# Neighbourhood attention by head pairs on two row halves, another split of the accumulator banks, and two more gate chunks ahead of attention, in a two-layer transformer trunk on one core

## The chip, the cores and the metric

The kernel runs on one core of a Trainium2 chip. The metric is the device time of one execution in microseconds (us). Before the change the median of three runs is 1344.7 us (1344.02 to 1344.84).

A core has five engines that run beside each other, each through its own instructions in order: TensorE (PE, with its weight loads listed as PEld), VectorE (DVE), ScalarE (ACT), GpSimd (POOL) and SyncE (SP), which here issues most of the loads. They wait for each other through semaphores. TensorE writes to PSUM, which has 8 banks of 128 × 512 f32 values.

## The reference

A trunk of two layers over 256 context tokens and 256 latent tokens, width 1024. Each layer has a mixer with two attentions in parallel and a feed-forward part. Cut to what matters:

```python
def mixer_proj(h, w_in, ...):
    p = h @ w_in                      # gates | c_q | c_kv | k_r | na q,k,v
    mq = rms_norm(c_q, g_qa) @ w_uq   # 8 heads of 96 (64 + 32 rotary)
    kv = rms_norm(c_kv, g_kva) @ w_ukv
    nq, nk, nv = ...                  # 8 heads of 64
    return gate_logits, mq, mk, mv, nq, nk, nv

# latent attention (MLA): latent queries see context + latent keys
y_mla = softmax(mq mk^T / sqrt(96)) mv
# neighbourhood attention (NA): a 4 x 16 window of the 4 x 64 grid, with a
# learned bias per head, and all context keys, in one softmax
s_win = nq k_win^T / 8 + bias;  s_ctx = nq k_ctx^T / 8
y_na  = softmax([s_win, s_ctx]) [v_win, v_ctx]
g = sigmoid(gate_logits)
y = (g[:1024] * (y_mla @ w_mla_o) + g[1024:] * (y_na @ w_na_o)) @ w_out
x = x + gate * y
x = x + gate2 * (relu(h2 @ w_ff1)**2 @ w_ff2)
```

In layer one the context tokens go through the same steps, seeing context alone. Layer two is the last, so only the latent tokens have queries, gates and a feed-forward part there.

## The kernel before

All inputs are f32. A weight tile is loaded by SP (`raw`), rounded by ScalarE to a high part (`whi`, L127), and VectorE makes the rest (`wlo`, L128). A product is three matmuls, high × high, low × high and high × low (`mm3`, L101 to L103), in a reduced f32 format that the trace calls fp32r. The four groups of 128 tokens are two of context (0, 1) and two of latent (2, 3); layer two takes queries from groups 2 and 3 only, so its gate matmuls have 256 columns where layer one's have 512.

The PSUM banks are shared by tag: A has three, B two, C two, D one (`BANKS`, L55). A tile waits until an earlier tile of its tag has been read.

Each layer runs through these stages: projections of `w_in` (c_kv, c_q, then keys, values and queries of MLA); the gate chunks that come ahead, `NG0 = 6` of 16 (a chunk is 128 of the gates' 2048 columns, 24 matmuls, drawn in the trace as `psB<-h,whi` ahead of attention and as `psA<-h,whi` later); MLA; the remaining `chunk_na` projections of NA; NA; the remaining gates; `w_mla_o`, `w_na_o`, `w_out`; the feed-forward part. The code is written for a scheduler that orders each engine's instructions by priority and by what is ready in its own plan. It draws projections in between MLA's steps and gate chunks in between NA's.

Attention before goes by head. `attend` (L816) takes the heads two at a time; for each, `prep` brings the transposed and split queries and keys (once per pair in NA), and in NA the head's bias: four loads on SP (L766), then an addition of the window mask on GpSimd (L767), into one of two `bias` buffers. `soft` (L784) goes over the tokens: three score matmuls into a bank of tag B, for latent tokens the bias added by VectorE (L778), the maximum (L787), the exponential on ScalarE (L796), reciprocal and scaling on VectorE (L798, L799), then transpositions of P on TensorE (L806) and the copies of the result (`PT`, L810 on ScalarE, L812 on VectorE). The value matmuls (L833) follow, head 1 and head 0 on the two column halves of the array. Head 1 of a pair starts after head 0. A head has 64 dimensions, so a score matmul of NA fills 64 of the array's 128 rows: head 0 of a pair lies on partitions 0 to 63 and head 1 on 64 to 127.

The context queries of layer one have 256 keys per token, the latent ones 512.

Of the kernel before, what the change touches and what calls it, by code (L numbers as in the profile page):

```python
# [37 lines left out]
NG0 = 6  # L38
# [7 lines left out]
def trunk(ctx: ExitStack, tc, t):  # L46
# [8 lines left out]
    BANKS = {"A": 3, "B": 2, "C": 2, "D": 1}  # L55
# [6 lines left out]
    def psx():  # L62
        cyc[0] += 1
        return ps("ABACBAC"[cyc[0] % 7])
# [316 lines left out]
    def load_xT(k):  # L381
        o = ps("AAABBABA"[k])
# [70 lines left out]
    for l in range(DEPTH):  # L453
# [16 lines left out]
        cqp = [ps("A"), ps("A"), ps("A"), ps("B"), ps("B"), ps("C") if l else ps("C")]  # L470
# [52 lines left out]
        def proj_b(load, nk, act_h, act_l, toks, N, evac, banks=("AA", "AA")):  # L523
# [3 lines left out]
            for p0 in range(0, len(toks), 2):  # L527
                pair = toks[p0:p0 + 2]
                outs = [ps(b)[:, :N] for b in banks[p0 // 2]]
                n = 0  # L530
                for wh, wl, ks in tiles:
                    for j, k in enumerate(ks):
                        for o, tk in zip(outs, pair):
                            cs = slice(tk * 128, (tk + 1) * 128)
                            mm3(o, act_h(k)[:, cs], act_l(k)[:, cs], wh[:, j], wl[:, j], n == 0, n == total - 1)
                        n += 1
                for o, tk in zip(outs, pair):
                    evac(tk, o)
# [31 lines left out]
        def rope(z, tab, lt, n):  # L570
# [7 lines left out]
            for half in range(2):  # L578
                zz = z[:, :, half * 16:(half + 1) * 16]
                aa = a[:, :, half * 16:(half + 1) * 16]  # L580
                bb = b[:, :, half * 16:(half + 1) * 16]
                nc.gpsimd.tensor_tensor(out=zz[:, :, 0:8], in0=aa[:, :, 0:8], in1=bb[:, :, 8:16], op=ALU.add)
                nc.gpsimd.tensor_tensor(out=zz[:, :, 8:16], in0=aa[:, :, 8:16], in1=bb[:, :, 0:8], op=ALU.add)
# [37 lines left out]
        proj_b(ckv_load, 3, H, Lo, [0, 1, 2, 3], KVL + RD, ckv_evac, ("CD", "AA"))  # L621
# [89 lines left out]

        gates(NG0, "B")

# [31 lines left out]
        na_pair = {}  # L745

        def prep_na(h):
            if h % 2 == 0:
                cs = slice(h * HD, (h + 2) * HD)
                o = ps("C")  # L750
                for tk in range(q0, 4):
                    nc.tensor.transpose(o[:, tk * 128:(tk + 1) * 128], nqk[:, tk, cs], rev if tk >= 2 else ident)
                qh, ql = qk_tile(), qk_tile()
                split_ps(qh[:, c_q], ql[:, c_q], o[:, c_q], gcn[:, l:l + 1])
                o = ps("C")
                for tk in range(4):
                    nc.tensor.transpose(o[:, tk * 128:(tk + 1) * 128], nqk[:, 4 + tk, cs], ident)
                kh, kl = qk_tile(), qk_tile()
                split_ps(kh, kl, o)
                na_pair[0] = (qh, ql, kh, kl)  # L760
            bias = ap.tile([128, 2, ROWS, GW], F32, tag="bias", name="bias", bufs=2)
            for row in range(ROWS):
                src = bass.AP(tensor=t["rpb"].tensor, offset=(l * NH + h) * RPB + (7 - row) * RW + 15 - (GW - 1),
                              ap=[[1, GW], [RW, ROWS], [1, GW]])
                pr = (row % 2) * 64
                nc.sync.dma_start(out=bias[pr:pr + 64, row // 2], in_=src)  # L766
            nc.gpsimd.tensor_tensor(out=bias.rearrange("p a i j -> p (a i) j"), in0=bias.rearrange("p a i j -> p (a i) j"),  # L767
# [48 lines left out]
        def attend(prep, score, vsel, ev, perm):  # L816
            groups = ([] if last else [([0, 1], LC, 0)]) + [([2, 3], TT, 1)]
            nxt = prep(0)
            for hp in range(NH // 2):
# [3 lines left out]
                for gi, (toks, K, st) in enumerate(groups):  # L823
# [6 lines left out]
                    for kt in range(nkt):  # L830
# [7 lines left out]
                        with tc.issue_after(first.ins):  # L838
                            av(0, ta)
# [260 lines left out]
```

## Time and profile before

| | us |
|---|---|
| median of 3 runs | 1344.7 |
| lowest, highest | 1344.02, 1344.84 |
| the profiled execution | 1344.34 |
| its span in the trace | 1342.6 |

The granted clock of TensorE averages 0.992 in it. The stages in that execution, by where the named instructions stand in the trace:

| us from the start | stage |
|---|---|
| 0 to 158 | layer one: modulation, norm, projections |
| 158 to 266 | MLA, with NA's projections in between |
| 280 to 369 | NA, with gate chunks in between |
| 369 to 486 | rest of the gates, `w_mla_o`, `w_na_o`, `w_out`, norm |
| to 843 | feed-forward |
| 843 to 926 | layer two: projections, six gate chunks |
| 926 to 989 | MLA |
| 989 to 1024 | rest of NA's projections |
| 1024 to 1090 | NA, with gate chunks in between |
| 1090 to 1145 | rest of the mixer |
| to the end | feed-forward |

In a row of the trace stands the start, the length, the engine, the line, the operation, the tiles (out<-in, buffer numbers left out) with rows and columns, and in brackets how long the engine stood idle before and what released it. TensorE works on several matmuls at once, so the length of one is more than what it adds; what it adds is read from one start to the next.

### The profile page before, as it was taken

The page shows a single profiled execution, that of the slowest core. Times are in us where ns is not written, and L with a number is a line of the kernel's source. Part 1 is how long each engine was busy: PE and PEld are TensorE (multiplying, and loading weights), DVE is VectorE, ACT ScalarE, POOL GpSimd, SP SyncE. Part 2 cuts the span into 40 slices and gives each one's busy share as a digit, 9 for nine tenths or more (in the row PEclk, how much of TensorE's full clock was granted, in tenths as well). Part 3 has the DMA queues.
Part 4 walks back from the last instruction along what each step waited for, and adds up shares of the span by engine and source line. Part 5 has one row for each costly group of instructions (what it writes and reads, how often), then busy time and mean ns, then how long its engine had stood idle before and what let it go on. Part 6 is the DMA issues. An engine that isn't in the chain of part 4 may idle for free.

```text
span 1342.6 us, 20389 instructions
## 1 busy us (share of the span) xinstructions
PE 1306.7 (97%) x7825; PEld 1098.5 (82%) x7825; DVE 863.4 (64%) x1462; ACT 586.5 (44%) x1061; POOL 275.8 (21%) x296
## 2 busy tenths in 40 slices
PE   6999999999999989999999999998999999999997
PEld 4698888976687868888888888898889789899896
DVE  4589377867885588887574334765854766755453
ACT  3455366445423344331423313564654544554442
POOL 3035403401005003210201100056040121221111
PEclk8999999999999999999999999999999999999999
DMA  9865411544477645465473344575134769656652
GB/s 277 285 151 165 151 32 32 157 113 85 93 261 235 202 144 165 150 187 173 133 212 96 101 125 150 167 191 150 32 87 97 121 216 273 170 163 189 189 187 94
DMA packets 245985, 208.01 MB, mean 155 GB/s; under 512 B 24496, under 2 KB 226992, under 8 KB 245504
## 3 DMA queue, kind: packets, MB, share of 16 engines
q1 hardware_dynamic: 235856, 190.16, 49.9%
q10 hardware_dynamic: 9520, 16.29, 3.4%
q8 instruction: 61, 1.00, 0.3%
q0 software_dynamic: 512, 0.27, 0.2%
q14 instruction: 36, 0.29, 0.1%
HBM read 195.15 MB, written 11.53 MB: 154 GB/s over the span
## 4 chain that ended last, share of the span: by engine, by line
PE 57%; issue 5%; DMA 2%; DVE 1%; POOL 1%; ACT 1%; SPq 0%; POOLq 0%; ACTq 0%; DVEq 0%
PE psA L103 8%; PE psA L102 8%; PE psA L101 8%; PE psB L101 5%; PE psB L102 5%; PE psB L103 5%; PE psC L101 4%; PE psC L103 4%; PE psC L102 4%; DMA bias<-in_rpb_dram 1%; PE psD L833 1%; PE psC L806 1%; DMA raw<-in_w_ff_dram 1%; PE psD L101 1%; PE psD L102 1%
## 5 line engine op out<-in xcount | busy, mean ns | idle before, releaser
L128 DVE TENSOR_TENSOR wlo<-raw,whi 128x1024 fp32r<-128x1024 f32 (+3 forms) x254 | 311.8, 1229 | 209.2 <-ACT whi L127 203.4
L127 ACT ACTIVATE whi<-raw 128x1024 fp32r<-128x1024 f32 (+3 forms) x254 | 261.1, 1029 | 376.2 <-PE psA L102 110.1
L233 DVE SCALAR_TENSOR_TENSOR ada<-raw,silu,ada 128x1024 f32<-128x1024 f32 (+1 forms) x105 | 123.7, 1211 | 19.4 <-DMA raw<-in_w_ada_dram 19.3
L102 PE MATMUL psA<-wlo,h 128*128 128x256 f32 (+2 forms) x416 | 123.5, 297 | 0.5 <-DVE wlo L128 0.5
L101 PE MATMUL psA<-whi,h 128*128 128x256 f32 (+2 forms) x416 | 123.2, 296 | 0.0
L103 PE MATMUL psA<-whi,h 128*128 128x256 f32 (+2 forms) x416 | 122.8, 296 | 0.0
L102 PE MATMUL psA<-h,whi 128*128 128x512 f32 (+1 forms) x312 | 110.0, 354 | 0.0
L103 PE MATMUL psA<-h,wlo 128*128 128x512 f32 (+1 forms) x312 | 109.5, 353 | 0.0
L101 PE MATMUL psA<-h,whi 128*128 128x512 f32 (+1 forms) x312 | 109.0, 358 | 0.1
L101 PEld LDWEIGHTS psA<-whi,h 128*128 128x128 f32 x416 | 79.7, 192 | 2.9 <-issue 0.8
L102 PEld LDWEIGHTS psA<-wlo,h 128*128 128x128 f32 x416 | 79.7, 192 | 2.4 <-DVE wlo L128 0.8
L103 PEld LDWEIGHTS psA<-whi,h 128*128 128x128 f32 x416 | 79.7, 192 | 1.9 <-issue 0.4
L983 POOL TENSOR_TENSOR fl<-s,fa 128x512 fp32r<-128x512 f32 (+1 forms) x32 | 38.3, 1198 | 176.6 <-ACT fa L982 176.6
L103 PE MATMUL psB<-h,wlo 128*128 128x512 f32 (+1 forms) x208 | 72.5, 349 | 0.0
L102 PE MATMUL psB<-h,whi 128*128 128x512 f32 (+1 forms) x208 | 72.5, 349 | 0.0
L101 PE MATMUL psB<-h,whi 128*128 128x512 f32 (+1 forms) x208 | 72.2, 350 | 0.0
L983 POOL TENSOR_TENSOR h<-s,h 128x512 fp32r<-128x512 f32 (+1 forms) x32 | 36.9, 1153 | 169.2 <-ACT h L982 169.2
L101 PEld LDWEIGHTS psA<-h,whi 128*128 128x128 f32 x312 | 58.3, 190 | 12.6 <-issue 6.3
L103 PEld LDWEIGHTS psA<-h,wlo 128*128 128x128 f32 x312 | 59.4, 190 | 10.0 <-issue 3.1
L767 POOL TENSOR_TENSOR bias<-bias,wmask 128x512 f32<-128x512 f32 x16 | 21.7, 1355 | 223.2 <-DMA bias<-in_rpb_dram 183.9
L102 PEld LDWEIGHTS psA<-h,whi 128*128 128x128 f32 x312 | 59.4, 190 | 9.8 <-issue 2.9
L101 PE MATMUL psA<-G,whi 128*128 128x512 f32 (+1 forms) x184 | 65.1, 354 | 0.0
(353 smaller groups left out, 3363.9 us busy)
## 6 DMA issues: line engine op xcount, KB each, us to landing
raw<-in_w_ff_dram SPq DMA_DIRECT2D x128, 512.0 KB, 4.2
raw<-in_w_ada_dram SPq DMA_DIRECT2D x62, 512.0 KB, 4.2
raw<-in_w_in_dram SPq DMA_DIRECT2D x56, 512.0 KB, 4.1
spare<-in_w_ada_dram SPq DMA_DIRECT2D x30, 512.0 KB, 7.2
raw<-in_w_out_dram SPq DMA_DIRECT2D x16, 512.0 KB, 6.3
raw<-in_w_in_dram SPq DMA_DIRECT2D x16, 384.0 KB, 5.4
xT_d<-xT SPq DMA_DIRECT2D x2, 2048.0 KB, 11.8
bias<-in_rpb_dram SPq DMA_DIRECT2D x64, 64.0 KB, 7.1
```

The costliest lines, as they stand in the source:

```text
L101: nc.tensor.matmul(out, sh, mh, start=first, stop=False)
L102: nc.tensor.matmul(out, sh, ml, start=False, stop=False)
L103: nc.tensor.matmul(out, sl, mh, start=False, stop=last)
L127: nc.scalar.activation(out=hi, in_=src, func=AF.Copy)
L128: nc.vector.tensor_tensor(out=lo, in0=src, in1=hi.bitcast(F32), op=ALU.subtract)
L233: nc.vector.scalar_tensor_tensor(out=a, in0=raw[:, c:c + w], scalar=sc, in1=a, op0=ALU.mult, op1=ALU.add)
L767: nc.gpsimd.tensor_tensor(out=bias.rearrange("p a i j -> p (a i) j"), in0=bias.rearrange("p a i j -> p (a i) j"), in1=wmask.unsqueeze(1).t ...
L806: nc.tensor.transpose(o[:, kt * 256 + i * 128:kt * 256 + (i + 1) * 128], pt[:, (kp * 2 + kt) * 128:(kp * 2 + kt + 1) * 128], perm if K == ...
L833: return nc.tensor.matmul(yo[z * 64:(z + 1) * 64, oc], vsel(kt, 2 * hp + z), tr[kt // 2][:, kt % 2, :], start=kt == 0, stop=kt == nkt - 1, ...
L983: nc.gpsimd.tensor_tensor(out=al[:, f, :], in0=s[:, :TQ], in1=ah[:, f, :].bitcast(F32), op=ALU.subtract)
```

## The change

It has these parts.

- `BANKS` goes from A 3, B 2, C 2, D 1 to A 2, B 3, C 2, D 1, and the places that take banks in turn are adapted: `psx`, `load_xT`, the `c_q` banks, `c_kv`, the last feed-forward part. `proj_b` takes two A banks and two B banks alternately for its token pairs. The NA chunks put both tokens of a pair in the two halves of one A bank, one token after the other.
- `NG0` becomes (6, 8): in layer two 8 of the 16 gate chunks come ahead of MLA.
- The rotary step on GpSimd makes its sums with two additions per call for four.
- MLA and NA get functions of their own. NA goes by head pair. `prep_na` brings queries, keys and both biases of a pair, with three `bias` buffers. The scores of both heads are issued in turn, head 1 and head 0, for each of the three terms, into two banks of tag B. The first of them can be moved by the scheduler, the others have a high priority and keep their order. Both heads' softmax then runs in one go.
- The value matmuls (`mix`) run over the key tiles backwards, and all but the first have a high priority and keep their order.

The diff, cut to its core:

```diff
-NG0 = 6
+NG0 = (6, 8)
-    BANKS = {"A": 3, "B": 2, "C": 2, "D": 1}
+    BANKS = {"A": 2, "B": 3, "C": 2, "D": 1}
-        return ps("ABACBAC"[cyc[0] % 7])
+        return ps("ABCBABC"[cyc[0] % 7])
...
-                outs = [ps(b)[:, :N] for b in banks[p0 // 2]]
+                if banks == "one":
+                    o = ps("A")
+                    outs = [o[:, i * N:(i + 1) * N] for i in range(2)]
+                else:
+                    turn[0] += 1
+                    outs = [ps(b)[:, :N] for b in (banks[p0 // 2] if banks else ("AA", "BB")[turn[0] % 2])]
...
-                nc.gpsimd.tensor_tensor(out=zz[:, :, 0:8], in0=aa[:, :, 0:8], in1=bb[:, :, 8:16], op=ALU.add)
-                nc.gpsimd.tensor_tensor(out=zz[:, :, 8:16], in0=aa[:, :, 8:16], in1=bb[:, :, 0:8], op=ALU.add)
+            for i in range(2):
+                nc.gpsimd.tensor_tensor(out=zz[:, :, :, i], in0=aa[:, :, :, i], in1=bb[:, :, :, 1 - i], op=ALU.add)
...
-        gates(NG0, "B")
+        gates(NG0[l], "B")
...
-            bias = ap.tile([128, 2, ROWS, GW], F32, tag="bias", name="bias", bufs=2)
+            for h in (2 * hp, 2 * hp + 1):
+                bias = ap.tile([128, 2, ROWS, GW], F32, tag="bias", name="bias", bufs=3)
...
+        def mix(yo, st, K, vsel, hp, ta, tb):
+            for kt in reversed(range(nkt)):
+                for z, tr in ((1, tb), (0, ta)):
+                    lead = z == 1 and kt == nkt - 1
+                    with nullcontext() if lead else tc.high_priority(2000):
+                        mm = nc.tensor.matmul(
+                            yo[z * 64:(z + 1) * 64, oc], vsel(kt, 2 * hp + z), tr[kt // 2][:, kt % 2, :],
+                            start=kt == nkt - 1, stop=kt == 0, tile_position=(0, z * 64))
+                    if not lead:
+                        tc.keep_in_program_order(mm)
...
+                def scores(os, tk, K, head):
+                    cs = slice(tk * 128, (tk + 1) * 128)
+                    for n, (q_, k_) in enumerate(((qh, kl), (ql, kh), (qh, kh))):
+                        for z in (1, 0):
+                            zs = slice(z * HD, (z + 1) * HD)
+                            lead = head and n == 0 and z
+                            with nullcontext() if lead else tc.high_priority(2000):
+                                mm = nc.tensor.matmul(os[z], q_[zs, cs], k_[zs, :K], start=n == 0, stop=n == 2)
+                            if not lead:
+                                tc.keep_in_program_order(mm)
...
+                        for tk in toks:
+                            banks = [ps("B"), ps("B")]
+                            scores(banks, tk, K, True)
+                            bs = [b[:, tk - 2].rearrange("p i j -> p (i j)") for b in biases]
+                            for z, pt in enumerate(softmax(list(zip(banks, bs)), K)):
+                                P[z].append(pt)
+                    if gi == len(groups) - 1 and hp < NH // 2 - 1:
+                        nxt = prep_na(hp + 1)
+                    ta, tb = (flip(p, K, rev) for p in P)
+                    mix(yo, st, K, vsel, hp, ta, tb)
```

The order of instructions on the engines moves with it. First TensorE in layer one, in NA, where the scores of the second head pair begin (scores are `psB<-qk`, gates `psA<-h,…`, value matmuls `psD<-PT,yv`); before:

```order
L101 MATMUL psB<-qk 128x256
L103 MATMUL psA<-h,wlo 128x512
L101 MATMUL psA<-h,whi 128x512
L102 MATMUL psA<-h,whi 128x512
L102 MATMUL psB<-qk 128x256
L103 MATMUL psB<-qk 128x256
L103 MATMUL psA<-h,wlo 128x512
```

and of the change, at the same place:

```order
L880 MATMUL psB<-qk 128x256 x12
L826 MATMUL psC<-rev,P 128x128 x6
L880 MATMUL psB<-qk 128x512
L102 MATMUL psA<-h,whi 128x512
L826 MATMUL psC<-rev,P 128x128 x4
```

The context scores of both heads and both tokens, spread among the gates before, now stand as twelve in a row.

Then TensorE at the first scores of NA in layer two, with buffer numbers; before:

```order
L101 MATMUL psB_9965<-qk_9948,qk_9939 128x512 [waits Activation_49]
L101 MATMUL psB_9978<-qk_9948,qk_9939 128x512
L102 MATMUL psA_10418<-h_7764,whi_10414 128x256
L103 MATMUL psA_10418<-h_7763,wlo_10415 128x256
L101 MATMUL psA_10418<-h_7763,whi_10414 128x256
...
L102 MATMUL psB_9965<-qk_9949,qk_9939 128x512 [waits DVE_49]
L103 MATMUL psB_9965<-qk_9948,qk_9940 128x512
L102 MATMUL psB_9978<-qk_9949,qk_9939 128x512
L103 MATMUL psB_9978<-qk_9948,qk_9940 128x512
```

and of the change:

```order
L880 MATMUL psB_9988<-qk_9971,qk_9961 128x512 [waits DVE_49]
L880 MATMUL psB_9987<-qk_9971,qk_9961 128x512
L880 MATMUL psB_9988<-qk_9970,qk_9962 128x512 [waits Activation_49]
L880 MATMUL psB_9987<-qk_9970,qk_9962 128x512
L880 MATMUL psB_9988<-qk_9970,qk_9961 128x512
L880 MATMUL psB_9987<-qk_9970,qk_9961 128x512
L880 MATMUL psB_10014<-qk_9971,qk_9961 128x512
```

The six matmuls of one token now alternate between two banks, that is between the two heads.

Last, VectorE in NA of layer two, around the adds of the second head pair, of the change. `bias_9980` is the second bias of pair one, whose buffer `bias_10061`, the second of pair two, takes over; the first row is the last that reads it:

```order
L782 TENSOR_TENSOR psB_10014<-psB_10014,bias_9980 128x256 [waits PE_49]
...
L796 TENSOR_SCALAR P_10027<-P_10027,ri_10033 128x512 [waits DVE_49]
L796 TENSOR_SCALAR P_10030<-P_10030,ri_10036 128x512 [waits DVE_49]
L782 TENSOR_TENSOR psB_10106<-psB_10106,bias_10055 128x256 [waits PE_49]
L784 TENSOR_REDUCE nm_10115<-psB_10106 128x1 [waits DVE_49]
L832 COPY PT_10079<-psC_10074 128x512 [waits PE_49]
L782 TENSOR_TENSOR psB_10107<-psB_10107,bias_10061 128x256 [waits DMAHW7_49,DMAHW0_49,Pool_49]
L795 RECIPROCAL ri_10126<-sm_10121 128x1 [waits Activation_49]
...
L782 TENSOR_TENSOR psB_10132<-psB_10132,bias_10055 128x256 [waits PE_49]
L832 COPY PT_10093<-psC_10088 128x512 [waits PE_49]
```

Twelve rows stand between the first row and the add of `bias_10061`, which waits for its loads and for GpSimd; between the corresponding rows of pair three there are 16, of pair four 11. Before, at the second pair, each head's bias was awaited in its own turn:

```order
L778 TENSOR_TENSOR psB_10040<-psB_10040,bias_9958 128x256 [waits PE_49]
L812 COPY PT_10003<-psC_9998 128x512 [waits PE_49]
...
L799 TENSOR_SCALAR P_10047<-P_10047,ri_10050 128x512 [waits DVE_49]
L778 TENSOR_TENSOR psB_10084<-psB_10084,bias_10021 128x256 [waits DMAHW5_49,DMAHW6_49,PE_49,Pool_49]
L128 TENSOR_TENSOR wlo_10585<-raw_10582,whi_10584 128x1024 [waits DMAHW2_49,Activation_49]
L812 COPY PT_10065<-psC_10060 128x512 [waits PE_49]
```

There a copy `PT` also stands behind a bias add. Ahead of MLA in layer two, TensorE has 192 gate matmuls where it had 144.

More of the change, by code (lines that the diff above doesn't have):

```diff
@@ L743, in score_mla @@
             mm3(o, qh[:QK, cs], ql[:QK, cs], kh[:QK, :K], kl[:QK, :K], True, True)
[L745 to L760, printed above, removed]
-            bias = ap.tile([128, 2, ROWS, GW], F32, tag="bias", name="bias", bufs=2)
[L762 to L767, printed above, removed]
-                                    in1=wmask.unsqueeze(1).to_broadcast([128, 2 * ROWS, GW]), op=ALU.add)
-            return na_pair[0] + (bias, (h % 2) * HD)
@@ L771, in score_na, with prep_na @@
[L771 to L780 removed]
+        def prep_na(hp):
+            cs = slice(2 * hp * HD, (2 * hp + 2) * HD)
+            o = ps("C")
+            for tk in range(q0, 4):
+                nc.tensor.transpose(o[:, tk * 128:(tk + 1) * 128], nqk[:, tk, cs], rev if tk >= 2 else ident)
+            qh, ql = qk_tile(), qk_tile()
+            split_ps(qh[:, c_q], ql[:, c_q], o[:, c_q], gcn[:, l:l + 1])
+            o = ps("C")
+            for tk in range(4):
+                nc.tensor.transpose(o[:, tk * 128:(tk + 1) * 128], nqk[:, 4 + tk, cs], ident)
+            kh, kl = qk_tile(), qk_tile()
+            split_ps(kh, kl, o)
+            biases = []
+            for h in (2 * hp, 2 * hp + 1):
+                bias = ap.tile([128, 2, ROWS, GW], F32, tag="bias", name="bias", bufs=3)
+                for row in range(ROWS):
+                    src = bass.AP(tensor=t["rpb"].tensor, offset=(l * NH + h) * RPB + (7 - row) * RW + 15 - (GW - 1),
+                                  ap=[[1, GW], [RW, ROWS], [1, GW]])
+                    pr = (row % 2) * 64
+                    nc.sync.dma_start(out=bias[pr:pr + 64, row // 2], in_=src)
+                nc.gpsimd.tensor_tensor(out=bias.rearrange("p a i j -> p (a i) j"),
+                                        in0=bias.rearrange("p a i j -> p (a i) j"),
+                                        in1=wmask.unsqueeze(1).to_broadcast([128, 2 * ROWS, GW]), op=ALU.add)
+                biases.append(bias)
+            return qh, ql, kh, kl, biases
@@ new lines, in softmax @@
+        def softmax(tiles, K):
+            nms, ss = [], []
+            for o, b in tiles:
+                if b is not None:
+                    nc.vector.tensor_tensor(out=o[:, LC:TT], in0=o[:, LC:TT], in1=b, op=ALU.add)
+                nm = small("nm", 1)
+                nc.vector.tensor_reduce(out=nm, in_=o, op=ALU.max, axis=AX, negate=True)
+                nms.append(nm)
+            out = []
+            for (o, b), nm in zip(tiles, nms):
+                pt = ap.tile([128, TT], F32, tag="P", name="P", bufs=4)
+                s = small("sm", 1)
+                nc.scalar.activation(out=pt[:, :K], in_=o, func=AF.Exp, bias=nm, scale=1.0, accum_out=s)
+                ss.append(s)
+                out.append(pt)
+            for pt, s in zip(out, ss):
+                ri = small("ri", 1)
+                nc.vector.reciprocal(out=ri, in_=s)
+                nc.vector.tensor_scalar(out=pt[:, :K], in0=pt[:, :K], scalar1=ri, scalar2=None, op0=ALU.mult)
+            return out
@@ L869, in evac @@
                                             op=ALU.mult)
-            proj_b(loader(w_in, 0, OFF_NA + part * 512 + half * 256, 256, 4, 8), 2, H, Lo, toks, 256, evac)
+            proj_b(loader(w_in, 0, OFF_NA + part * 512 + half * 256, 256, 4, 8), 2, H, Lo, toks, 256, evac, "one")
             if (part, half) in ((0, 1), (2, 0), (2, 1)):
```

105 lines of the change are left out of this document (53 added, 52 removed).

## The prediction

> **What bounds the kernel now.** I read the page first, then a table of windows by stage, then the chain of waits inside the last neighbourhood stage, then TensorE's rows one by one.
>
> ```profile
> PE 1306.7 (97%) x7825; PEld 1098.5 (82%) x7825; DVE 863.4 (64%) x1462; ACT 586.5 (44%) x1061; POOL 275.8 (21%) x296
> ...
> PE 57%; issue 5%; DMA 2%; DVE 1%; POOL 1%; ACT 1%; SPq 0%; POOLq 0%; ACTq 0%; DVEq 0%
> ```
>
> TensorE is busy for 97% of the span and holds most of the chain, so a change pays if it takes time out of TensorE's stream, or closes one of the few holes in it. The windows show where those can be (start and end in us, length, then busy time of PE, PEld, DVE, ACT, POOL, granted clock, DMA share, GB/s):
>
> ```profile
> 280.00:369.00 89.00, 88.96 (x471) 59.30 (x471) 68.74 (x153) 45.67 (x105) 7.76 (x6) 1.00 0.44 85
> ...
> 843.00:926.00 83.00, 82.16 (x640) 75.60 (x639) 58.29 (x115) 51.84 (x111) 36.79 (x55) 1.00 0.65 182
> ...
> 1024.00:1090.00 66.00, 64.55 (x435) 49.99 (x434) 49.87 (x98) 34.27 (x73) 7.87 (x6) 1.00 0.62 123
> ```
>
> 280–369 is neighbourhood attention (NA) of layer one, 843–926 the projections of layer two, 1024–1090 NA of layer two. VectorE has 20 us to spare in the first and 16 in the last. Busy is not useful, though. These are successive matmuls of a score in layer two (start, length, tile):
>
> ```profile
> 1028.23 0.28 PE L103 MATMUL psA<-h,wlo 128*128 128x256 f32 x1
> 1028.44 0.50 PE L102 MATMUL psB<-qk 64*128 64x512 f32 x1
> 1028.77 0.39 PE L103 MATMUL psB<-qk 64*128 64x512 f32 x1
> 1029.01 0.39 PE L102 MATMUL psB<-qk 64*128 64x512 f32 x1
> 1029.24 0.39 PE L103 MATMUL psB<-qk 64*128 64x512 f32 x1
> 1029.56 0.39 PE L101 MATMUL psA<-h,whi 128*128 128x256 f32 x1
> 1029.78 0.28 PE L102 MATMUL psA<-h,whi 128*128 128x256 f32 x1
> 1029.90 0.28 PE L103 MATMUL psA<-h,wlo 128*128 128x256 f32 x1
> ```
>
> Starts tell the price. A score matmul (64 rows of the array, 512 columns) takes 0.23 us from the next (1029.01 to 1029.24), a gate matmul of 256 columns 0.12 (1029.78 to 1029.90). Where the stream passes from full rows to half rows, 0.21 stands in place of 0.12 and then 0.33 in place of 0.23; on the way back 0.32 and 0.22 in place of 0.23 and 0.12. So each switch costs about **0.2 us**, on top of the work.
>
> The chain of waits in the same stage (start, length, what) is not TensorE's alone:
>
> ```profile
> 1064.29 0.77 DVE psB L778 x2
> 1065.12 0.60 SPq L766
> 1065.77 2.19 SPq L766
> ...
> 1068.66 7.53 DMA bias<-in_rpb_dram
> 1076.35 1.29 POOL bias L767
> 1077.66 0.43 DVE psB L778
> ```
>
> A bias buffer is freed by the VectorE add that reads it (ends 1065.06), refilled by four loads from SP, masked by GpSimd (ends 1077.64), and only then may the add of a later head run: **12.6 us** for one round.
>
> **The change, part by part.**
>
> *Score pairs.* The number of score matmuls stays; the two heads of a pair now alternate on the two row halves. That two such matmuls run side by side is not shown before, but column halves are:
>
> ```profile
> 945.41 0.38 PE L806 MATMUL psC<-ident,P 128*128 128x128 f32 x2
> 945.72 1.95 PE L833 MATMUL psD<-PT,mv 128*64 128x256 f32 x16
> ...
> 1050.65 0.88 PE L806 MATMUL psC<-rev,P 128*128 128x128 f32 x6
> ```
>
> In the second row are 8 value matmuls (two records each) in 1.95 us, 0.12 for each record. Plain f32 transpositions of 128 columns, which are not tiled, cost (0.88 − 0.38) / 4 = 0.125 each, so records of 256 columns would need about 0.25, 4.0 us for 16 in line; at 1.95 the two column halves run together. I take it that row halves do the same; the bounds are no gain at all and a half of all score time. A token has 6 matmuls per pair; the order puts the first alone and five later, 1 + 2 + 1 more slots, so 4 slots for 6 (3 where the first is not cut off, 6 if nothing runs together). Layer one: 8 token groups of 512 columns save 16 slots × 0.23 = 3.6 us, and 4 batches of 12 with 256 columns need 6 slots each, 24 × 0.12 = 2.9. Layer two: 28 slots for 48, 20 × 0.23 = 4.6.
>
> The Trainium skill, "TensorE: Matmul & The Clock Gate", section "Part 3: Packing small matmuls — row/col tiling", gives 3.07× for four row tiles, and says that a weight load overlaps a running matmul only if its row group differs. An estimate from that figure is 6 / (2 × 0.77) = 3.9 slots for a token's 6, and the sum would hardly move. The trace does not bear the second half out: in the score rows above successive loads go to the same rows and the matmuls still stand 0.23 apart.
>
> *Fewer switches.* Counting in the two orders where TensorE passes between full, half-row and half-column work gives 76 before and 46 after in NA of layer one, 42 and 27 in layer two. At 0.2: −6.0 and −3.0 us. The value batches also no longer fall apart into four and four. Bounds: nothing, and 0.3 per switch, were the transpositions beside a score to lose as well.
>
> *Two more gate chunks ahead in layer two.* 48 matmuls at 0.12 = 5.8 us leave the NA stage and go ahead of the latent attention, where TensorE now stands still:
>
> ```profile
> 926.90 0.49 PE L735 MATMUL psC<-ident,mqk 128*96 128x128 f32 x3
> 930.84 0.32 PE L735 MATMUL psC<-ident,mqk 128*96 128x128 f32 x1 [3.46 <-POOL mqk L701]
> ...
> 931.64 0.42 PE L103 MATMUL psA<-whi,h 128*128 128x256 f32 x1
> 931.86 0.42 PE L101 MATMUL psA<-whi,h 128*128 128x256 f32 x1
> ```
>
> and the same in windows:
>
> ```profile
> 934.00:935.00 1.00, 1.00 (x6) 0.95 (x5) 0.00 (x0) 0.13 (x1) 0.00 (x0) 0.54 0.00 0
> ```
>
> The last key tile comes 3.46 us late from GpSimd. Right after the hole the same 256-column matmuls stand 0.22 apart, not 0.12, and the granted clock is 0.54 still at 934–935: about 3.4 us at half clock, so 1.7 us more. 5.8 us of cover ends at 932.5, past the 930.8 at which GpSimd is done, so hole and slow stretch go: 5.8 − 3.5 − 1.7 = **+0.6** at that place. Late next would be the two chunks' weights: 2 × 512 KB more before 926, 3.7 us at the 280 GB/s that 182 at a share of 0.65 means; the DMA engines have 29 idle us there, and ACT and VectorE some 25 to split them in. Bounds 0.6 − 1.7 and 0.6 + 3.7.
>
> *The biases.* Both biases of a head pair are now asked for together with three buffers for four in use, so the second one of each next pair must wait for an add of the present pair. VectorE runs in order, so all that stands behind that add waits as well, a PT copy among it that the flips and value matmuls on TensorE need. First of six rounds in layer two (the last is in the chain above):
>
> ```profile
> 1029.20 0.90 DVE L778 TENSOR_TENSOR psB<-psB,bias 128x256 f32<-128x256 f32 x2 [1.25 <-PE psB L103]
> ...
> 1039.63 1.27 POOL L767 TENSOR_TENSOR bias<-bias,wmask 128x512 f32<-128x512 f32 x1 [30.92 <-DMA bias<-in_rpb_dram]
> ```
>
> 1030.10 to 1040.90 is 10.8 us; the mean of the six is 11.9. VectorE's rows between the freeing add and the waiting one, at the means of this stage:
>
> ```profile
> L128 DVE TENSOR_TENSOR wlo<-raw,whi 128x1024 fp32r<-128x1024 f32 x10 | 12.3, 1230 | 3.6 <-ACT whi L127 3.4
> L787 DVE TENSOR_REDUCE nm<-psB 128x1 f32<-128x512 f32 x16 | 10.7, 681 | 0.1
> L799 DVE TENSOR_SCALAR P<-P,ri 128x512 f32<-128x512 f32 x16 | 9.2, 584 | 0.2
> L778 DVE TENSOR_TENSOR psB<-psB,bias 128x256 f32<-128x256 f32 x16 | 6.7, 428 | 5.8 <-POOL bias L767 3.3 <-PE psB L103 2.5
> L812 DVE COPY PT<-psC 128x512 f32<-128x512 f32 x8 | 5.5, 685 | 2.2 <-PE psC L806 2.2
> L721 DVE TENSOR_TENSOR qk<-psC,qk 128x512 fp32r<-128x512 f32 x4 | 2.7, 684 | 0.0
> L798 DVE RECIPROCAL ri<-sm 128x1 f32<-128x1 f32 x16 | 2.5, 156 | 0.1
> L724 DVE SCALAR_TENSOR_TENSOR qk<-psC,gcn,qk 128x256 fp32r<-128x256 f32 x4 | 1.9, 483 | 1.4 <-ACT qk L723 1.3
> L893 DVE TENSOR_TENSOR ym<-psD,ym 128x256 fp32r<-128x256 f32 x4 | 1.7, 424 | 2.9 <-ACT ym L892 2.9
> ```
>
> Pair two of layer two: 3 scales 1.75, 2 adds 0.86, 3 maxima 2.04, a split 1.23, 2 reciprocals 0.31, a copy 0.69, together 6.9; 11.9 − 6.9 = **5.0 us** uncovered. Pair three: 16 rows (2 splits, 2 maxima, 2 copies, 3 scales, 3 reciprocals, and four others) are 9.4; 2.5 uncovered. Pair four: 11 rows, 6.3; 5.6 uncovered. Sum 13.1, which I charge to TensorE in full, since its own filler is thinner by the 5.8 us moved ahead. Bounds: 0 (TensorE has other rows that long) and 3 × 12.6 = 38. I take 13.1, nearer the low end, because the rows ahead of each add are fixed by the order. On SP the four loads of each such bias stand in line too: behind those of pair two are a load of w_na_o and the next bias, which no one needs before the stage's end or the next pair, so they cost nothing. The old holes of this window (66.00 − 64.55 = 1.45) go with the old order.
>
> A hole also costs clock, and this is where a page and a row differ:
>
> ```profile
> 1144.56 0.44 PE L202 MATMUL psC<-ident,ada 128*128 128x128 f32 x2 [2.41 <-ACT ada L197]
> ...
> 1147.00:1148.00 1.00, 1.00 (x9) 0.60 (x4) 0.00 (x0) 0.38 (x1) 0.07 (x1) 0.50 1.02 303
> ```
>
> Here 2.41 us of idleness was followed by a clock of 0.50. So I add 1.7 us for each of the two long waits, **3.4**, and leave the short one as a bound (5.1). The Trainium skill, same page, section "Why this matters for your kernels", asks for no idle gaps over about 3 us; by it alone the two long waits count and the sum is the same 3.4, but the row shows that 2.41 is enough, so the measurement decides and 5.1 stays open.
>
> In layer one a head pair takes 89 / 4 = 22 us, about 19 after, and the context scores lie between, so a round of 12 is covered; VectorE's room there falls from 20 to about 8 us, for which I charge 2 (0 to 8).
>
> *Banks, alternating token pairs, two rope adds fewer, one bank for a chunk pair.* TensorE is 82.16 of 83 busy in the projections, so at most 0.8 is to be had there, and an evacuation that comes late would cost as much. I take 0, with ±2.
>
> **The sum.** Layer one: −3.6 − 2.9 − 6.0 + 2.0 = −10.5. Layer two ahead of attention: +0.6. NA of layer two: −5.8 − 4.6 − 3.0 − 1.45 + 13.1 + 3.4 = +1.7. Together −8.2. The profiled execution took 1344.34, 0.36 under the median of the runs; 1344.34 − 8.2 = 1336.1, on the scale of the median 1336.5. I say **1336**; with the small unknowns 1331 to 1341.
>
> **The rivals.**
>
> *The bias rounds are hidden* (22%). For it: the stage holds eight gate chunks, some 23 us of matmuls that need no softmax. Against it: the chain above already passes through two rounds, and the adds waited 3.3 us for GpSimd's bias (L778's row). All hidden: 13.1 + 3.4 less, 1319.5; a good half of it, 1327.
>
> *The row halves run one after the other* (13%). Then 3.6 + 2.9 + 4.6 = 11.1 comes back, 1347; part of the last 4.6 would lie inside the bias waits, so 1343 to 1347. For it: no row shows two row halves at once. Against it: column halves do.
>
> *Switches are not what the excess is* (10%): 0.2 belongs to another wait that stays. 9.0 comes back, 1345. This is the case where the change does not do what it says.
>
> *Slower: the bias round binds in layer one also* (10%). Three rounds there, with cover like pair four's 6.3, leave 3 × 5.6 = 16.8 uncovered instead of my 2: 1336 + 14.8 = 1351. It decides once VectorE's rows ahead of the second add, context softmax included, come to under 11.9 us.
>
> **How the numbers follow.** Forecast 45%, the rivals as above. The range reaches from the middle of the first rival to the upper end of the second: 1323 to 1347; the far ends of the first and last stay out. Under about 0.2%, 2.7 us, a difference cannot be told from none. Faster by more: the forecast, the first rival and 3 of the second's 13 points, 0.70; within it the second's other points but 2 and the third rival, 0.18; slower the last rival and those 2, 0.12.
>
> **What would show it.** Score matmuls of two heads starting a few ns apart, 0.23 to the next couple; a granted clock of 1 and no GpSimd hole ahead of the latent attention; in NA of layer two waits of 3 to 6 us at the add, put down to GpSimd's bias, with TensorE idle behind them; NA of layer one near 78 us, that of layer two near 68. I am wrong if score starts stay 0.23 apart one by one, if NA of layer two falls to 55, or if layer one shows the bias waits.

## The result, and the profile after

The changed kernel takes 1335.5 us (median of 4 runs, 1332.7 to 1338.3) against 1344.4 for the kernel before (4 runs): a ratio of 0.9925, 95% interval 0.9902 to 0.9949, so some 9 to 10 us faster. Run again on another occasion (e0 below) it gave 0.9912, interval 0.9885 to 0.9939. Single runs of one kernel scatter by several us here, the kernel before from 1340.7 to 1349.7 in 19 runs, so the medians are compared, and differences of a few us are read from the stages of the traces.

The profiled execution took 1332.72 us, its span is 1330.9. The page of the changed kernel, busy time by engine and the chain that ended last:

```profile
PE 1287.8 (97%) x7825; PEld 1091.4 (82%) x7825; DVE 858.2 (64%) x1462; ACT 583.8 (44%) x1061; POOL 277.5 (21%) x280
...
PE 75%; DVE 7%; DMA 6%; POOL 2%; ACT 2%; issue 2%; SPq 1%; POOLq 0%; ACTq 0%; DVEq 0%
```

On the chain VectorE and DMA have grown from 1% and 2% to 7% and 6%. Something other than TensorE now sets part of the end. The windows of neighbourhood attention (NA) in layer one, of the way from the first transposition of latent attention (MLA) to its first score in layer two, and of NA in layer two, cut where those instructions stand (start and end, length, busy of PE, PEld, DVE, ACT, POOL, granted clock, DMA share, GB/s), tell where:

```profile
282.00:355.30 73.30, 71.97 (x447) 50.04 (x444) 64.42 (x153) 43.75 (x104) 6.98 (x5) 1.00 0.40 77
...
921.80:925.40 3.60, 3.02 (x26) 2.77 (x25) 2.22 (x3) 2.28 (x4) 1.27 (x2) 1.00 0.65 194
1013.50:1079.40 65.90, 56.14 (x391) 43.63 (x389) 45.04 (x92) 31.57 (x68) 6.38 (x5) 0.90 0.52 107
```

The same three in the kernel before:

```profile
280.70:368.30 87.60, 87.56 (x462) 57.98 (x460) 67.74 (x151) 44.88 (x104) 7.76 (x6) 1.00 0.44 84
...
926.70:934.50 7.80, 4.34 (x28) 4.08 (x26) 2.30 (x3) 2.28 (x4) 3.94 (x4) 0.81 0.57 163
1024.20:1088.40 64.20, 62.75 (x420) 48.20 (x419) 48.27 (x93) 33.72 (x72) 7.87 (x6) 1.00 0.62 124
```

NA of layer one lost 14.3 us, but 3.6 of them are no gain: 16 gate matmuls of 0.227 us now come after the stage (the stretch from NA's end to the last modulation went from 118.9 to 122.4). The hole ahead of MLA is gone, and its clock of 0.81 is 1.00. NA of layer two is *longer* by 1.7 us although TensorE is busy for 6.6 us less in it, and its clock fell from 1.00 to 0.90: there the whole gain was given back. Layer two's mixer as a whole, from the modulation ahead of it to the one behind it, is as long as it was. These are its windows, each time up to MLA's first score and in full, before:

```profile
849.00:934.50 85.50, 81.34 (x608) 77.13 (x607) 57.95 (x111) 52.02 (x111) 40.48 (x60) 0.98 0.65 176
849.00:1150.60 301.60, 291.16 (x2189) 258.62 (x2188) 196.87 (x378) 159.63 (x323) 79.12 (x97) 0.99 0.56 147
```

and changed:

```profile
837.30:925.40 88.10, 85.92 (x654) 81.72 (x654) 59.94 (x113) 54.13 (x115) 42.34 (x53) 1.00 0.68 183
837.30:1138.90 301.60, 284.90 (x2187) 255.55 (x2187) 194.10 (x378) 158.08 (x322) 80.04 (x89) 0.98 0.55 147
```

So in these two executions nearly all that the change won lies in layer one's mixer: from MLA's first transposition to the last modulation 328.6 us before and 318.1 after.

The gain first. TensorE at the first scores of NA in layer two, changed kernel (start, length, tile; rows of one kind are joined):

```profile
1017.50 0.28 PE L101 MATMUL psA<-h,whi 128*128 128x256 f32 x1
1017.71 1.19 PE L880 MATMUL psB<-qk 64*128 64x512 f32 x7
1018.83 0.66 PE L760 MATMUL psC<-ident,nqk 128*128 128x128 f32 x4
```

Seven score matmuls take 1.12 us from the first start to the next kind's. One by one at 0.23 they need over 1.6. The single starts in the trace are 3 to 6 ns apart within a couple; from the first couple to the second it is 0.33 us, as behind the switch to half rows in the kernel before, and 0.23 from there on: the two row halves work at the same time. Counting a couple as one slot, the scores of NA have 24 slots of 256 columns and 32 of 512 in layer one, and 29 in layer two.

Then what was given back. VectorE's bias adds that waited for a bias, one in layer one and three in layer two, and ahead of the wait at 1047.30 the add that freed its buffer (in brackets the idle time and what ended it):

```profile
307.48 0.43 DVE L782 TENSOR_TENSOR psB<-psB,bias 128x256 f32<-128x256 f32 x1 [1.86 <-POOL bias L771]
...
1034.39 0.43 DVE L782 TENSOR_TENSOR psB<-psB,bias 128x256 f32<-128x256 f32 x1 [4.68 <-POOL bias L771]
1035.85 0.42 DVE L782 TENSOR_TENSOR psB<-psB,bias 128x256 f32<-128x256 f32 x1
...
1047.30 0.76 DVE L782 TENSOR_TENSOR psB<-psB,bias 128x256 f32<-128x256 f32 x2 [0.73 <-POOL bias L771]
...
1063.55 0.43 DVE L782 TENSOR_TENSOR psB<-psB,bias 128x256 f32<-128x256 f32 x1 [5.47 <-POOL bias L771]
```

and TensorE at the same places:

```profile
1032.45 0.28 PE L103 MATMUL psA<-h,wlo 128*128 128x256 f32 x1
1036.92 3.68 PE L846 MATMUL psD<-PT,yv 128*64 128x256 f32 x16 [4.19 <-DVE PT L832]
...
1064.63 3.68 PE L846 MATMUL psD<-PT,yv 128*64 128x256 f32 x16 [5.23 <-DVE PT L832]
```

The three waits in layer two come at pairs two, three and four, and TensorE stands still behind the first and the last, released by a PT copy, which waits on VectorE behind the add. The value batch after each hole takes 3.68 us, where the same 16 records took 1.95 in the prediction's row: the clock. By windows of 10 us, and for the first batch alone:

```profile
1030.00:1040.00 10.00, 5.81 (x36) 3.67 (x34) 4.85 (x12) 3.61 (x8) 2.29 (x2) 0.76 0.68 120
...
1060.00:1070.00 10.00, 5.37 (x25) 2.98 (x26) 4.46 (x11) 1.83 (x5) 1.26 (x1) 0.66 0.25 70
...
1037.00:1041.00 4.00, 4.00 (x18) 2.10 (x19) 2.24 (x5) 1.12 (x3) 1.27 (x1) 0.50 0.63 121
```

Summing starts to next starts by kind of work over the two NA stages accounts for their length to within 0.2 us (us; gates with the number of matmuls in the stage; a wait is what a start comes later than the kind of work ahead of it explains, counted where two starts lie over 0.7 us apart):

| | scores | transpositions | gates | values | waits | length |
|---|---|---|---|---|---|---|
| layer one, before | 23.1 | 14.2 | 38.7 (139) | 11.6 | 0.0 | 87.6 |
| layer one, after | 14.0 | 14.1 | 32.2 (123) | 11.6 | 1.6 | 73.4 |
| layer two, before | 14.6 | 9.1 | 31.4 (218) | 7.7 | 1.6 | 64.2 |
| layer two, after | 9.5 | 10.3 | 25.5 (189) | 11.0 | 9.7 | 65.9 |
| layer two, e3 (below) | 9.0 | 9.9 | 25.7 (189) | 7.5 | 0.0 | 52.1 |

### The profile page after: what moved, and what is told of

It is laid out like the page before. It is cut to its first block, busy times and chain, and to the rows that moved or that the text cites. A ratio compares the mean times of both kernels' runs of the same rounds, so it can differ in the third digit from the quotient of the medians.

```text
span 1330.9 us, 20341 instructions
## 1 busy us (share of the span) xinstructions
PE 1287.8 (97%) x7825; PEld 1091.4 (82%) x7825; DVE 858.2 (64%) x1462; ACT 583.8 (44%) x1061; POOL 277.5 (21%) x280
## 4 chain that ended last, share of the span: by engine, by line
PE 75%; DVE 7%; DMA 6%; POOL 2%; ACT 2%; issue 2%; SPq 1%; POOLq 0%; ACTq 0%; DVEq 0%
PE psA L103 9%; PE psA L102 9%; PE psA L101 9%; PE psB L101 9%; PE psB L102 9%; PE psB L103 9%; PE psC L101 4%; PE psC L103 4%; PE psC L102 4%; PE psD L846 2%; DMA bias<-in_rpb_dram 2%; PE psC L826 2%; DVE wlo L128 2%; DMA raw<-in_w_ada_dram 1%; DVE ada L233 1%
## 5 line engine op out<-in xcount | busy, mean ns | idle before, releaser
L102 PE MATMUL psA<-wlo,h 128*128 128x256 f32 (+2 forms) x400 | 118.2, 296 | 1.7 <-DVE wlo L128 1.7
L101 PE MATMUL psA<-whi,h 128*128 128x256 f32 (+2 forms) x400 | 117.6, 294 | 0.0
L103 PE MATMUL psA<-whi,h 128*128 128x256 f32 (+2 forms) x400 | 117.6, 294 | 0.0
L102 PE MATMUL psB<-h,whi 128*128 128x512 f32 (+1 forms) x272 | 94.3, 348 | 0.0
L103 PE MATMUL psB<-h,wlo 128*128 128x512 f32 (+1 forms) x272 | 94.1, 347 | 0.0
L101 PE MATMUL psB<-h,whi 128*128 128x512 f32 (+1 forms) x272 | 93.3, 349 | 0.0
L103 PE MATMUL psA<-h,wlo 128*128 128x512 f32 (+1 forms) x256 | 90.6, 355 | 0.0
L101 PE MATMUL psA<-h,whi 128*128 128x512 f32 (+1 forms) x256 | 90.5, 359 | 0.1
L102 PE MATMUL psA<-h,whi 128*128 128x512 f32 (+1 forms) x256 | 89.9, 352 | 0.0
L101 PEld LDWEIGHTS psA<-whi,h 128*128 128x128 f32 x400 | 76.3, 191 | 1.9
L103 PEld LDWEIGHTS psA<-whi,h 128*128 128x128 f32 x400 | 76.3, 191 | 1.7
L103 PE MATMUL psC<-G,wlo 128*128 128x256 f32 (+1 forms) x200 | 64.2, 321 | 0.0
L102 PE MATMUL psC<-G,whi 128*128 128x256 f32 (+1 forms) x200 | 64.2, 321 | 0.0
L101 PE MATMUL psC<-G,whi 128*128 128x256 f32 (+1 forms) x200 | 64.1, 322 | 0.0
L101 PE MATMUL psB<-G,whi 128*128 128x512 f32 (+1 forms) x168 | 59.0, 351 | 0.0
## 6 DMA issues: line engine op xcount, KB each, us to landing
xT_d<-xT SPq DMA_DIRECT2D x2, 2048.0 KB, 11.8
```

The source lines that it names most:

```text
L101: nc.tensor.matmul(out, sh, mh, start=first, stop=False)
L102: nc.tensor.matmul(out, sh, ml, start=False, stop=False)
L103: nc.tensor.matmul(out, sl, mh, start=False, stop=last)
```

## The experiments

All times are medians with the ratio to the kernel before, run on the same chip. e0 to e3, e4 to e7 and e8 to e10 had a chip each, so across these groups the ratios compare better than the medians.

**e0: the changed kernel again.**

> The changed kernel once more, beside its variants on the same chip: about 9 us under the kernel before. The spread of its four earlier times was 5.6 us (1332.72 to 1338.29), so the variants are to be set against this run and not against those.

1331.7 us, ratio 0.9912 (0.9885 to 0.9939).

**e1: eight gate chunks alone**, on the kernel before.

```diff
-NG0 = 6
+NG0 = (6, 8)
-        gates(NG0, "B")
+        gates(NG0[l], "B")
```

> The kernel before with nothing but 8 gate chunks ahead of attention in layer two. Theory: the 3.46 us wait for GpSimd and the 1.7 us lost to the half clock behind it go, the 5.8 us of gate matmuls only change their place, so about 5 us less than before (1339 to 1340 where before has 1344.4). Rival: the hole turns up elsewhere, because the neighbourhood stage has less to fill its bias waits with; then 0 to 2 us less.

1345.2 us, ratio 1.0015 (0.9998 to 1.0031): nothing gained, as the rival had it. The hole did go. Its windows, again MLA's first steps and NA:

```profile
932.90:935.90 3.00, 2.99 (x27) 2.79 (x25) 1.87 (x3) 2.29 (x4) 0.00 (x0) 1.00 0.76 229
1025.40:1089.90 64.50, 61.71 (x408) 46.80 (x406) 46.48 (x92) 32.56 (x70) 8.51 (x6) 1.00 0.62 123
```

7.8 us became 3.0 at a clock of 1.00. But NA, with 26 gate matmuls (3.1 us) less, is as long as before, 64.5 for 64.2: 14 matmuls of the output projections (2.3 us), drawn in ahead of their time, and waits of 2.7 us for 1.6 took the place. Behind NA, where the kernel before waits for no weight tile longer than 0.41 us, TensorE now does:

```profile
1098.87 0.38 PE L101 MATMUL psC<-ym,whi 128*128 128x256 f32 x1 [1.93 <-ACT whi L127]
...
1105.50 0.39 PE L101 MATMUL psC<-ym,whi 128*128 128x256 f32 x1 [2.71 <-ACT whi L127]
```

So a good part of the 4.8 us turned up again as waits further on. Layer two's mixer is 299.7 us long for 301.6 in this execution, which is the fastest of the ten (1342.83); that the median gains nothing is not explained further.

**e2: six chunks** in the changed kernel.

```diff
-NG0 = (6, 8)
+NG0 = (6, 6)
```

> The changed kernel with 6 gate chunks ahead in layer two, as before. Theory: the waits for the second bias are fixed by VectorE's order and stay, so the hole ahead of the latent attention comes back and the time is 5 us above the changed kernel. Rival: two more chunks in the neighbourhood stage (5.8 us) fill the bias waits, so the time is the same or up to 2 us less.

1333.5 us, ratio 0.9922 (0.9900 to 0.9943), 1.8 above e0, which is less than either's scatter (ten runs from 1331.3 to 1342.7). By the times this settles nothing. The trace says what it did not do: NA of layer two holds 189 gate matmuls as in the changed kernel and is 65.3 us long, with 9.1 us of waits, and the 48 others follow after it. The order was fixed ahead of the run, and it put none of this work into the waits. The hole ahead of MLA did come back, 5.01 us of waiting for GpSimd, and MLA's first steps took 10.7 us at a clock of 0.68 where the changed kernel has 3.6. So the traced execution bears the theory out, with a mixer of 308.5 us in layer two for 301.6; but it took 1341.41, the slowest but one of its ten, and how much of that stands behind the median is not shown.

**e3: no bias waited for in layer two.** The second bias of pairs two to four goes into the space of MLA's values, which are no longer needed.

```diff
-                bias = ap.tile([128, 2, ROWS, GW], F32, tag="bias", name="bias", bufs=3)
+                if last and h >= 3 and h % 2:
+                    if h == 3:
+                        vb[:] = [ap.tile([128, 4, 2, ROWS, GW], F32, tag="v", name="vbias", bufs=1)]
+                    bias = vb[0][:, h // 2]
+                else:
+                    bias = ap.tile([128, 2, ROWS, GW], F32, tag="bias", name="bias", bufs=3)
```

> The changed kernel, but in layer two the second bias of head pairs two to four goes into space that the latent attention no longer needs, so that no bias waits for an add of the present pair. Theory: TensorE's two waits in the neighbourhood stage (4.2 and about 4.3 us) and the half clock behind each (1.7) go, about 12 us less than the changed kernel; VectorE's adds wait under 1 us for a bias. Rival: VectorE (46 us busy in 67) or the softmax chain holds TensorE at the same places, 3 us less or nothing.

1320.0 us, ratio 0.9829 (0.9800 to 0.9857): 11.7 us under e0, as the theory said. What VectorE's bias adds waited for, and the NA window of layer two:

```profile
  POOL bias L778: 1.9, 1
```

```profile
1016.60:1068.70 52.10, 51.79 (x391) 41.39 (x390) 45.17 (x92) 31.54 (x68) 3.40 (x2) 1.00 0.47 120
```

The one wait left is in layer one. NA of layer two went from 65.9 to 52.1 us, TensorE is busy in 51.8 of them, and the clock is back at 1.00. This kernel beats both others.

**e4: the scores of the two heads in line**, on e3.

```diff
-                    for n, (q_, k_) in enumerate(((qh, kl), (ql, kh), (qh, kh))):
-                        for z in (1, 0):
+                    for z in (1, 0):
+                        for n, (q_, k_) in enumerate(((qh, kl), (ql, kh), (qh, kh))):
```

> The kernel of e3 with the scores of the two heads of a pair issued one head after the other instead of in turn, everything else kept. Theory (two row halves run side by side): the slots rise from 24 to 36 of 256 columns and from 32 to 48 of 512 in layer one, from 28 to 42 in layer two, 12 x 0.12 + 16 x 0.23 + 14 x 0.23 = 8.3 us above e3, of which 5.1 in the neighbourhood stage of layer one. Rival (the gain comes from the contiguous order alone): within 1 us of e3.

1320.9 us, ratio 0.9838 (0.9816 to 0.9860): by the times the rival, but these tell little here: the intervals of e3 and e4 overlap over some 5 us. The trace shows that the experiment had not undone what it was meant to undo. TensorE in layer two:

```profile
1041.27 0.98 PE L887 MATMUL psB<-qk 64*128 64x512 f32 x6
1042.19 0.66 PE L833 MATMUL psC<-rev,P 128*128 128x128 f32 x4
1042.77 0.96 PE L887 MATMUL psB<-qk 64*128 64x512 f32 x3
1043.67 0.55 PE L833 MATMUL psC<-rev,P 128*128 128x128 f32 x3
```

Six matmuls, three of head 1 issued ahead of three of head 0, are over as fast as three: 0.92 us to the next kind from the first row, 0.90 from the third. The single starts stand in couples 10 ns apart. In all four context batches of layer one and at three places in layer two the two heads' scores followed each other directly and still ran together. Elsewhere other work lay between them, or (twice in layer two) the second head's first one started 0.1 us after the other's last, and the pairs were gone: 48 slots of 512 columns for 32 in layer one, and 39 for 29 in layer two. The scores' time by starts rose from 13.9 to 17.8 us in layer one, and from 9.0 to 11.0 in layer two: 5.9 us of the 8.3 expected. Of that, the stages show 2.2 and 0.8, because in layer one 1.6 us of waiting was covered by it, and 7 gate matmuls (0.8) left NA of layer two.

**e5: pairs that can be torn apart**, on e3.

```diff
-                            lead = head and n == 0 and z
+                            lead = z
```

> The kernel of e3 with the first score matmul of each of the three terms free to be moved, so that other work comes in between. By the order that gives 9 and 7 more switches between full and half rows, and 6 x 0.12 + 24 x 0.23 = 6.2 us of slots in which no pair forms. Theory (a switch costs 0.2): 6.2 + 3.2 = 9.4 us above e3. Rival (switches cost nothing): 6.2 above. Third (the scheduler only moves work that TensorE would have waited for anyway): under 2.

1325.7 us, ratio 0.9866 (0.9837 to 0.9895), 5.7 above e3 (5.0 by the ratios, whose intervals just overlap). The scores take 19.2 and 11.8 us, 8.1 more together, and the 1.6 us of waits in layer one are covered. By the times that lies near the second expectation and below the first. The lost slots come to the 6.2 us expected, so 1.9 of the 8.1 us are left for the 16 added switches, 0.12 each. It tells that the pinning is worth having.

**e6: the kernel before without bias waits** in layer two.

```diff
-            bias = ap.tile([128, 2, ROWS, GW], F32, tag="bias", name="bias", bufs=2)
+            if last and h >= 2 and h % 2 == 0 or last and h == 3:
+                if h == 2:
+                    vb[:] = [ap.tile([128, 4, 2, ROWS, GW], F32, tag="v", name="vbias", bufs=1)]
+                bias = vb[0][:, {2: 0, 3: 1, 4: 2, 6: 3}[h]]
+            else:
+                bias = ap.tile([128, 2, ROWS, GW], F32, tag="bias", name="bias", bufs=2)
```

> The kernel before with the biases of layer two taken from the same free space as in e3, the rest as it was. Theory: the neighbourhood stage of layer two was held by bias rounds already, since 5.8 us less matmuls in e1 did not shorten it; the adds' waits of 3.3 us go and the time falls by 2 to 5 us. Rival: TensorE held it (62 of 64 us busy); no change.

1342.6 us, ratio 1.0003 (0.9987 to 1.0019): no change by the times. NA of layer two is 62.6 us long with no waits, 1.6 less. So the bias rounds cost the kernel before 1.6 us there, and the 12 us of e3 are a cost that the change had made.

**e7: the bank part alone**, on the kernel before: the hunks on `BANKS`, `psx`, `load_xT`, the `c_q` and `c_kv` banks, `proj_b` with "one", and "BCCD".

> The kernel before with the bank part of the change alone: tags of 2, 3, 2 and 1 banks, token pairs in alternate banks, one bank for the pairs of the neighbourhood projections. Theory: this term is 0 within 2 us. Rival: the third bank of tag B is what lets the scores of a token start early, and a good part of the 9 to 13 us of gain is there without pairs, 4 us or more.

1339.9 us, ratio 0.9974 (0.9956 to 0.9993): about 3.5 us faster, between the two expectations. The scores fell from 23.1 to 21.7 us in layer one and from 14.6 to 12.2 in layer two with no pairing in the code: with a third B bank the next head's scores more often stand right behind the present one's, and its trace has 9 couples of 256 columns and 7 of 512 in the two stages, where the kernel before has 2. That this is where the 3.5 us come from is not shown: NA of layer two is as long as before, 64.0 us, with 26 gate matmuls fewer and 6.0 us of waits for 1.6.

**e8: value matmuls not pinned**, on e3, in the old loop.

```diff
-            for kt in reversed(range(nkt)):
-                for z, tr in ((1, tb), (0, ta)):
...
+            for kt in range(nkt):
...
+                first = av(1, tb)
+                with tc.issue_after(first.ins):
+                    av(0, ta)
```

> The kernel of e3 with the value matmuls issued as in the kernel before (key tiles forward, none pinned). By the order the value batches of the neighbourhood stages fall into 14 and 8 pieces for 8 and 4, with 7 and 6 more switches; slots and score pairs stay the same. Theory (0.2 us per switch): 1.4 and 1.2 us more in the two stages, 2.6 in all, to be read in the stages since 2.6 is near what the times can tell. Rival (a switch costs nothing where work is queued): the stages stay within 0.5 us of e3's 73.5 and 52.1.

1318.7 us, ratio 0.9812 (0.9795 to 0.9830), which is e3's within the intervals. In the stages the value matmuls take 12.5 and 8.1 us for 11.6 and 7.5. The lengths are 70.7 and 50.7, with 16 gate matmuls of 0.227 and 20 of 0.12 fewer in them; with these, 74.3 and 53.1, 0.9 and 1.0 over e3. So 13 more switches cost 1.9 us, 0.15 each: the theory's sign, three quarters of its size. For the whole kernel the pinned value batches bring nothing that can be measured.

**e9: six chunks, and no bias waits** (e3 with the edit of e2).

> The kernel of e3 with 6 gate chunks ahead in layer two. With the bias waits gone TensorE has no hole in the neighbourhood stage, so two chunks cost the same 5.8 us there as ahead of attention. Theory: what is left is the hole for GpSimd ahead of the latent attention (3.5 us or more) and the half clock behind it (1.7), 5 us above e3. Rival: the scheduler finds other filler for that hole, within 1 us of e3.

1323.7 us, ratio 0.9849 (0.9826 to 0.9872), 3.7 above e3, or 2.7 by the ratios, whose intervals overlap. TensorE ahead of MLA:

```profile
920.51 0.32 PE L741 MATMUL psC<-ident,mqk 128*96 128x128 f32 x1 [3.46 <-POOL mqk L707]
```

The very hole of the kernel before is back, 3.46 us, and MLA's first steps take 7.2 us for 3.6, with a clock of 0.88. Layer two's mixer is 291.7 us long for 286.6 in e3. So with the bias waits gone the two chunks are worth 3 to 5 us, where e1 shows none by the times; by its trace e1 lost a good part again to waits behind the hole.

**e10: the old bank split with pairs**, on e3: the bank hunks undone, except "one".

> The kernel of e3 with the bank split of the kernel before (3, 2, 2, 1), so that the two score banks of one token are all of tag B. Theory: the next token's scores wait for both exponentials of the present one; VectorE and ScalarE need some 3.5 us for the two heads (2 adds 0.86, 2 maxima 1.36, 2 exponentials 1.4), which gates fill in layer one and not wholly in layer two; 2 to 6 us above e3. Rival: gates fill it, within 1 us of e3 in both neighbourhood stages.

1329.6 us, ratio 0.9886 (0.9869 to 0.9902), some 8 to 10 us above e3: more than the theory allowed, and not where it looked. In layer one, from MLA's first transposition to the last modulation before the feed-forward part, the profiled run needs 323.8 us where e3 has 320.5. The two NA stages themselves show no waits, with 30 more gate matmuls drawn into the first, and with the added work taken off they are 74.9 and 52.4 us long for 73.4 and 52.1. There the rival came nearer: other work fills the time in which the score banks are read. The way from the modulation to MLA in layer two takes 88.3 us for 84.1. In the rest of the mixer in layer two TensorE waited for weight tiles:

```profile
1086.93 0.39 PE L101 MATMUL psC<-ym,whi 128*128 128x256 f32 x1 [1.57 <-ACT whi L127]
...
1094.92 0.39 PE L101 MATMUL psC<-ym,whi 128*128 128x256 f32 x1 [2.71 <-ACT whi L127]
```

In e3's profile no wait of that stretch is longer than 1.09 us. But the profiled run of e10 was the slowest of its five (1336.9), so only a part of the 8 to 10 us is located.

## Why the prediction came out right

The forecast was 1336; the result is 1335.5. By its terms:

- **Score pairs and fewer switches in layer one**, −12.5. Scores −9.1 us, and the gates' time above 0.227 each (7.1 before, 4.3 after) −2.8: together −11.9. The 24 and 32 slots of the trace are 10.1 us, where the kernel before had 16.7, so pairs are 6.6 of it, as forecast; 5.3 are left for 30 switches, 0.18 each. e8 gives 0.15 us per switch and e5 0.12, for 0.2.
- **New waits in layer one**, +2: 1.6 measured.
- **Two chunks ahead**, +0.6: this was too cheap. From the modulation to MLA's first score in layer two it is 85.5 us before and 88.1 after, +2.6 (e1 has 86.6, e3 87.7, e0 89.3). The hole and its half clock went, 4.2 us of MLA's first steps for the 5.2 reckoned, and the projections ahead of them grew by 6.8 for 5.8. e1, e2 and e9 show the hole going and coming.
- **Pairs and switches in layer two**, −7.6: scores −5.1, and gates above 0.12 each −2.4.
- **Chunks taken out of NA**, −5.8: 29 gate matmuls fewer in the stage, 19 fewer after it.
- **Bias waits**, forecast 5.0, 2.5 and 5.6 uncovered on VectorE: 4.68, 0.73 and 5.47. Both parts of each difference were too large: from the add that frees the buffer to the waiting one it took 11.0, 11.0 and 11.4 us where I had 11.9, and VectorE's rows between took 6.0, 8.0 and 5.6 where I had 6.9, 9.4 and 6.3, since successive rows overlap. At pairs two and four the two errors nearly cancel, which is luck; at pair three VectorE also waited 2.4 us for other work, so that only 0.73 was left. On TensorE waits rose from 1.6 to 9.7, +8.1 against 13.1 − 1.45.
- **Half clock** behind the two long waits, +3.4: scores, transpositions and values took 0.5, 0.4 and 3.5 us more than in e3, 4.4. e3 took both terms away and won 11.7 us, so that they are shown and not only argued.

These come to −8.5 us, near the forecast −8.2 and the 8.8 between the medians. That is luck in part: the chunks were 2.0 too cheap, the half clock 1.0, the waits 3.5 too dear. The two profiled executions are 11.6 apart (1332.72 and 1344.34). Of what is left, 2.2 us lie in layer one's feed-forward part, 361.7 before and 359.5 after, where kernels with the same code differ by as much (360.7 in e0, 362.0 in e2), and 1.6 in MLA and the projections behind it in layer two; ahead of layer one's MLA 1.0 was lost. NA of layer one is 73.3 us and not near 78, because of the 16 gate matmuls that left it; NA of layer two is 65.9 for 68.

- **Banks and the rest**, 0 within 2: this term was mis-sized. The bank split alone is worth about 3.5 us (e7, 0.9 to 5.9), and undoing it in e3 costs 8 to 10 (e10). I had it as a small thing beside the pairs. In e7 the scores fall by 1.4 and 2.4 us without any pairing in the code, so a part of what stands above under pairs may be the banks'. What e10 loses lies outside its NA stages as far as it is located, and is not shown to be a loss of pairs.

The prediction also said that no row of the kernel before shows two row halves at once. That was wrong; its trace holds one such place, in NA of layer one:

```profile
349.88 0.28 PE L103 MATMUL psB<-qk 64*128 64x256 f32 x1
349.89 0.39 PE L102 MATMUL psB<-qk 64*128 64x512 f32 x1
```

Two matmuls on half rows start some 10 ns apart, one of them the last of a 256-column score, the other out of the next. With it, the rival of row halves in line would have had far less than 13%.

The rivals: that the bias rounds are hidden falls by the 12.7 us that VectorE's four waits for GpSimd's bias add up to; that the halves run in line falls by the starts; that switches are not what the excess is falls by the gates, which lost 2.8 and 2.4 us of time above their price as 30 and 15 switches went, and by e8, where 13 more cost 1.9. The prediction named a bias wait in layer one as a sign of being wrong. There is one, of 1.86 us on VectorE, but not the three long ones of that rival, and TensorE's 1.6 us lie within the 2 that were charged. The rule of the Trainium skill on idle gaps ("TensorE: Matmul & The Clock Gate", section "Why this matters for your kernels") agrees here: holes of 4.19 and 5.23 us were followed by half clock, 0.50 from 1037 to 1041.

What stays open: where all of e10's loss lies and where e7's gain does, why e1's median gains nothing, what e2's hole costs in a usual execution, and whether a switch costs 0.12 or 0.2 us. That TensorE could have been given other work in the bias waits was not tried.

## What to carry to other kernels

When heads are grouped, so are their loads: a pair that asks for two buffers at once needs the buffers of two pairs, and one short means that every pair waits for its predecessor in a queue where everything else stands behind. Look at what the engine in order has between the row that frees a buffer and the row that waits for its refill; that sum against one refill told these waits to within half a microsecond at two of three places, though with errors in both that happened to cancel. And closing a hole is worth only what does not come back as waits further on: the same two chunks closed the same hole in e1 and in e3, and gave nothing by the times in the one and about 3 us, with overlapping intervals, in the other (against e9).

## What the runs showed that was not expected

Two half-row score streams need not be issued in turn: three matmuls of one head followed by three of the other ran as couples 10 ns apart (e4), so the second head's first matmul started ahead of the first head's second, which had been issued earlier. And about a third of the time lost to a hole can come after it: the two holes in NA of layer two are 9.4 us of idleness, and the work behind them took 4.4 us more than in e3, 3.68 us for 1.95 in each value batch.
